# Order of the token operands in the output projection of an encoder step: sums ahead of squares, squares on ScalarE

## The chip, the cores and the metric

The kernel runs on one core of a Trainium2 chip. A core has a matrix engine (PE, with its weight loads shown apart as PEld), a vector engine (DVE), an activation engine (ACT), a general engine (POOL) and an engine that issues transfers (SP). Each works through its own list of instructions in order; semaphores hold an instruction until what it needs is there. Matmuls write to banks of PSUM, everything else lives in SBUF. The metric is the device time of one execution in microseconds, as the median of several runs.

## The reference

One layer of an encoder for 512 prompt frames behind 16 meta tokens, and 64 frames of a running stream. What matters here is the second half of the layer:

```python
mix = jnp.concatenate([o_d.reshape(B, L, D_DIFF), o_m.reshape(B, L, D_MLA)], axis=-1)
x = x + mix @ lp['w_out']
h = rmsnorm(x, lp['norm_ffn_g'])
x = x + (jax.nn.silu(h @ lp['ffn_w_gate']) * (h @ lp['ffn_w_up'])) @ lp['ffn_w_down']
```

`D_MODEL` is 2048, `D_FF` 5632, all in float32. After the meta tokens are dropped, 576 tokens (64 + 512) go through this part.

## The kernel before

Tokens lie along the free dimension, channels on the 128 partitions. A float32 product is made of three products of a faster format (fp32r): every operand is split into a high part (a cast on ACT) and a low part (source minus high part, a subtraction on DVE). `split` and `operand` issue such a pair of instructions.

The program has three phases. Streams of projections and attention come first; the output projection's first half (`mix_out`) runs among them. The third phase begins with the output projection's second half: 16 iterations `i`, one for each block of 128 channels of x, each of 2 half-iterations with 4 weight chunks. A half-iteration loads a 128x512 block of `w_out` (`wr`), splits it (`wh` on ACT, `wl` on DVE; two buffers each, fetched two half-iterations ahead), and runs 24 matmuls (`mm3`, line 205): for each chunk `wh` times `mh`, `wh` times `ml`, `wl` times `mh`, over two halves of 288 tokens. Here `mh` and `ml` are the split attention outputs. At the end of an iteration DVE adds the two sums to `x`, ACT makes `xg`, x scaled by the gain of the next norm, POOL squares x and accumulates the squares in `sq2` (lines 1198 to 1201), and SP stores x.

The feed-forward part that follows uses a Winograd scheme: a product of 2x2 blocks takes 7 products instead of 8. For it, each pair of channel blocks (iterations 2m and 2m+1, eight pairs m) needs seven operands of 128x288: four are quarters of the two `xg` or sums of them, and all seven are split. `token_operands` (line 1048) writes them down once the odd iteration's `xg` is there: operands 1, 2 and 3 are the quarters b11, b21 and b22; 5 is b12 - b11, 6 is b22 - 5, 4 is b21 - 6, 7 is b22 - b12. POOL makes the sums (lines 1060 to 1072, tiles `bs`), in place, so that a sum waits until the one before it has been split. The operands stay in SBUF as tiles `b{p}_{m}` of the pool `bc`.

Behind the loop, `winograd` (matmuls at lines 1155 and 1159) makes the first gate product over pairs 0 to 3 and then over pairs 4 to 7, in the order of products 1, 2, 4, 5, 6, 3, 7; the weights' sums come from POOL (line 1124) and DVE, and `wh`, `wl` again from ACT and DVE. The memory of its weight tiles is that of `mh` and `ml`, which the loop releases.

The order on PE is the order in which the program is written. ACT, DVE and POOL in this stage are not pinned: the framework's scheduler places their instructions by its own estimates of when they become ready, so the order in the program is only one of its inputs. Helpers record one line for all their instructions (125 for ACT, DVE and SP), so tiles tell them apart.

Of the kernel before, what the change touches and what calls it, by code (L numbers as in the profile page):

```python
# [11 lines left out]
F32 = mybir.dt.float32  # L12
F32R = mybir.dt.float32r
AF = mybir.ActivationFunctionType
ALU = mybir.AluOpType
# [4 lines left out]
P = 128  # L20
# [7 lines left out]
TQ = NS + SEQ  # L28
QH = TQ // 2
# [102 lines left out]
def encoder_step(  # L132
# [8 lines left out]
    V, S, Q, G = Engine(tc, nc.vector), Engine(tc, nc.scalar), Engine(tc, nc.sync), nc.gpsimd  # L141
# [10 lines left out]
    def load(dst, src):  # L152
        Q.dma_start(dst, src)

    def store(dst, src):
        Q.dma_start(dst, src)
# [8 lines left out]
    def f32(ap):  # L165
        return ap.bitcast(F32)
# [20 lines left out]
    def weights(src, kcs, cols, dup=False, pool=None):  # L187
        pool = pool or wp
        wr = pool.tile([P, kcs, cols], F32, name="wr", tag="wr", bufs=WR_BUFS)
        if dup:  # L190
            half = cols // 2
            for i in range(2):
                load(wr[:, :, i * half:(i + 1) * half], src)
        else:
            load(wr, src)
        wh = pool.tile([P, kcs, cols], F32R, name="wh", tag="wh", bufs=WH_BUFS)
        wl = pool.tile([P, kcs, cols], F32R, name="wl", tag="wl", bufs=WH_BUFS)
        split(wh, wl, wr)
        return wh, wl

    def mm3(outs, wh, wl, xh, xl, start, stop):
        n = len(outs)
        for p, (w, x) in enumerate(((wh, xh), (wh, xl), (wl, xh))):
            for i in range(n):
                PE.matmul(outs[i], w, x[i], start=start and p == 0, stop=stop and p == 2)  # L205

    def halves(ap):
        n = ap.shape[1] // 2
        return [ap[:, 0:n], ap[:, n:2 * n]]
# [131 lines left out]
    with ExitStack() as ph:  # L341
# [33 lines left out]
        with tc.tile_pool(name="xn", bufs=1) as xn, tc.tile_pool(name="xc", bufs=1, side="right") as xc:  # L375
# [127 lines left out]
            for j, (o, n) in enumerate(tok):  # L503
                b = o // TH
# [507 lines left out]
    def pool(name, side="left"):  # L1012
        cm = tc.tile_pool(name=name, bufs=1, side=side)
        return cm.__enter__(), lambda: cm.__exit__(None, None, None)

    bc, close_bc = pool("bc", "right")
    rw, close_rw = pool("rw", "right")
    sq2 = rw.tile([P, TQ], F32, name="sq2", tag="rows", bufs=2)
    rb2 = rw.tile([P, TQ], F32, name="rb2", tag="rows", bufs=2)
    operands = {}  # L1020
    ORDER = (1, 2, 4, 5, 6, 3, 7)
# [6 lines left out]
    def pin(ins):  # L1028
        if pinned[0]:
            tc.keep_in_program_order(ins)  # L1030
# [3 lines left out]
    def operand_tile(m, p):  # L1034
        b = bc.tile([P, 2, QH], F32R, name=f"b{p}_{m}")
        operands[m, p] = (b[:, 0, :], b[:, 1, :])
        return b

    def operand(m, p, src):
        operand_tile(m, p)  # L1040
        hi, lo = operands[m, p]
        pin(S.activation(hi, src, AF.Copy))
        pin(V.tensor_tensor(lo, src, f32(hi), op=ALU.subtract))

    def quarters(b1, b2):
        return b1[:, 0:QH], b1[:, QH:TQ], b2[:, 0:QH], b2[:, QH:TQ]

    def token_operands(pool, m, b1, b2):

        b11, b12, b21, b22 = quarters(b1, b2)  # L1050

        def sum_tile():
            return pool.tile([P, QH], F32, name="bs", tag="bs", bufs=2)

        operand(m, 1, b11)
        yield
        operand(m, 2, b21)
        yield
        t = sum_tile()
        pin(G.tensor_tensor(t, b12, b11, op=ALU.subtract))  # L1060
        operand(m, 5, t)
        yield
        pin(G.tensor_tensor(t, b22, t, op=ALU.subtract))
        operand(m, 6, t)
        yield
        pin(G.tensor_tensor(t, b21, t, op=ALU.subtract))
        operand(m, 4, t)
        yield
        operand(m, 3, b22)
        yield  # L1070
        t = sum_tile()
        pin(G.tensor_tensor(t, b22, b12, op=ALU.subtract))
        operand(m, 7, t)
        yield

    def load_raw(pool, src, r0, nk, c0, bufs, tag="raw"):
        r = pool.tile([P, nk, 256], F32, name="raw", tag=tag, bufs=bufs)
        load(r, src[r0:r0 + nk * P, c0:c0 + 256].rearrange("(k p) c -> p k c", p=P))
        return r
# [3 lines left out]
    def pmt():  # L1083
        return pm.tile([P, 512], F32, name="m", tag="m")
# [80 lines left out]
    ma, close_ma = pool("ma", "right")  # L1165
    mx, close_mx = pool("mx")
    mixh, mixl = [], []
    for h in range(H):
        m = ma.tile([P, TQ], F32, name="x", tag="x", bufs=3)
# [3 lines left out]
        split(mixh[h], mixl[h], m)  # L1173
    ws = {}

    def fetch(n):
        if n < 2 * KC:
            i, r0 = n // 2, 1024 + n % 2 * 512
            ws[n] = weights(w_out[r0:r0 + 512, i * P:(i + 1) * P].rearrange("(k p) c -> p k c", p=P), 4, P, pool=ma)

    for n in range(2):
        fetch(n)
    for i in range(KC):
        x = ma.tile([P, TQ], F32, name="x", tag="x", bufs=3)
        load(x, x1spill[i])
        ps = [pmt()[:, 0:QH] for _ in range(2)]
        for hf in range(2):
            wh, wl = ws.pop(2 * i + hf)
            for k in range(4):
                mm3(ps, wh[:, k, :], wl[:, k, :],  # L1190
                    halves(mixh[4 * hf + k]), halves(mixl[4 * hf + k]), hf + k == 0, hf + k == 4)
            fetch(2 * i + hf + 2)
        for xi, pi in zip(halves(x), ps):
            V.tensor_tensor(xi, xi, pi, op=ALU.add)
        xg = ma.tile([P, TQ], F32, name="xg", tag="xg", bufs=2)
        S.activation(xg, x, AF.Copy, scale=gF[:, i:i + 1])
        if i == 0:
            G.tensor_tensor(sq2, x, x, op=ALU.mult)
        else:
            G.tensor_tensor(rb2, x, x, op=ALU.mult)  # L1200
            G.tensor_tensor(sq2, sq2, rb2, op=ALU.add)
        store(x2spill[i], x)
        if i % 2:
            for _ in token_operands(ma, i // 2, xe, xg):
                pass
        xe = xg
        if i == 2:
            raw0 = load_raw(rw, w_gate, 0, 8, 0, 1)

    close_mx()  # L1210
    fr, close_fr = pool("fr")
# [161 lines left out]
    for u in range(FC // 2):  # L1373
        out = {}
        for which, wsrc in (("g", w_gate), ("u", w_up)):
            first = turn == 0
            raws = []
            for hf in range(2):
                if turn:
                    rp, bufs = (rw, 1) if turn % 3 == 0 else (fr, 2)  # L1380
# [57 lines left out]
        if u < FC // 2 - blocks[-1]:  # L1438
            b11, b12, b21, b22 = quarters(w[:, 0, :], w[:, 1, :])
            t = g.rearrange("p f (h c) -> p (f h) c", h=2)  # L1440
# [117 lines left out]
    for bi, n in enumerate(blocks):  # L1558
# [32 lines left out]
        else:  # L1591
# [6 lines left out]
            sums, free = itertools.cycle(free[0:3]), free[3:]  # L1598
# [93 lines left out]
```

## Time and profile before

| | |
|---|---|
| median of 3 runs | 2481.91 us (2481.80 to 2481.93) |
| the profiled execution | 2478.58 us, span 2476.8 us |
| PE busy over the span | 2409.9 us (97%) |
| POOL busy over the span | 733.8 us (30%) |
| the projection's second half | about 842.7 to 959.3 us of the span |
| first gate product | from 960.1 us |

In the rows of a timeline the columns are start and length in microseconds, engine, line, operation, output and inputs by the program's names, shapes and count; brackets hold the idle time just before on that engine and what ended it. In the waits the columns are who waited for whom, the total in microseconds, how often, and the longest. In rows of groups they are busy time and mean nanoseconds of one, and idle time before. `PE m L205` are the projection's matmuls, `wl<-wr,wh` a weight's low part, `b<-xg` and `b<-bs` an operand's parts.

### The profile page before, as it was taken

What the parts mean: (1) busy time and instruction counts of PE and PEld (TensorE: products, weight loads), DVE (VectorE), ACT (ScalarE), POOL (GpSimd) and SP (SyncE); (2) the same over time, 40 slices, a digit from 0 to 9 for tenths busy, and PEclk for the clock granted to TensorE, in tenths of its full rate; (3) what the DMA queues carried; (4) which work ended last, traced back from release to release, by engine and by line L of the source; (5) the groups of instructions that cost most, each with busy time, mean ns of one, the idle gap of its engine ahead of it and who ended that gap; (6) DMA issues with size and microseconds to landing.
All of it is one profiled execution on the core that took longest, in us unless ns stands there. A gap on an engine that the chain in (4) does not pass through costs nothing.

```text
span 2476.8 us, 44895 instructions
## 1 busy us (share of the span) xinstructions
PE 2409.9 (97%) x17697; PEld 2364.3 (95%) x17697; DVE 1781.8 (72%) x2831; ACT 1159.4 (47%) x2212; POOL 733.8 (30%) x590
## 2 busy tenths in 40 slices
PE   8999999999999999999999999999999999999998
PEld 6999999988999888999999999999999999999998
DVE  5555555556556567778878888788787988888874
ACT  5444444334444444445555455555554433333345
POOL 0000000000000165554555545545444322222223
PEclk9999999999999999999999999999999999999999
DMA  7533222334232454324444344334443965645332
GB/s 218 146 93 85 82 81 79 89 92 149 85 100 80 148 157 134 120 96 144 155 136 142 129 146 160 128 133 147 141 158 127 310 218 191 228 154 176 105 111 86
DMA packets 336485, 338.05 MB, mean 136 GB/s; under 512 B 25827, under 2 KB 279658, under 8 KB 336274
## 3 DMA queue, kind: packets, MB, share of 16 engines
q1 hardware_dynamic: 335714, 333.12, 42.1%
q8 instruction: 139, 2.28, 0.4%
q0 software_dynamic: 560, 2.06, 0.2%
q14 instruction: 72, 0.59, 0.1%
HBM read 265.21 MB, written 72.61 MB: 136 GB/s over the span
## 4 chain that ended last, share of the span: by engine, by line
PE 58%; DVE 1%; POOL 1%; DMA 1%; ACT 0%; issue 0%; DVEq 0%; POOLq 0%; SPq 0%
PE m L1155 38%; PE m L1159 19%; PE m L205 1%; DMA raw<-in_ffn_w_down 1%; DVE b L125 0%; PE m L1522 0%; DVE wl L125 0%; ACT b L125 0%; POOL b L1509 0%; POOL ws L1124 0%; POOL c L1327 0%; PE m L1536 0%; POOL b L1504 0%; ACT y L125 0%; DVE y L125 0%
## 5 line engine op out<-in xcount | busy, mean ns | idle before, releaser
L1155 PE MATMUL m<-b,wh 128*128 128x288 f32 x7168 | 1048.6, 295 | 4.9 <-ACT wh L125 2.6
L1155 PEld LDWEIGHTS m<-b,wh 128*128 128x128 f32 x7168 | 984.4, 189 | 7.3 <-ACT wh L125 4.9
L1159 PE MATMUL m<-b,wl 128*128 128x288 f32 x3584 | 579.3, 297 | 2.2 <-DVE wl L125 2.2
L1124 POOL TENSOR_TENSOR ws<-raw 128x512 f32<-128x512 f32 (+1 forms) x258 | 367.4, 1432 | 546.0 <-DVE wl L125 289.0
L1159 PEld LDWEIGHTS m<-b,wl 128*128 128x128 f32 x3584 | 513.6, 188 | 3.2 <-DVE wl L125 3.2
L125 ACT ACTIVATE wh<-ws 128x512 fp32r<-128x512 f32 (+1 forms) x340 | 283.5, 846 | 394.8 <-PE m L1155 250.4
L125 DVE TENSOR_TENSOR wl<-ws,wh 128x512 fp32r<-128x512 f32 (+1 forms) x340 | 388.8, 1154 | 93.8 <-ACT wh L125 93.5
L125 DVE TENSOR_TENSOR wl<-raw,wh 128x512 fp32r<-128x512 f32 x387 | 359.0, 953 | 7.5 <-ACT wh L125 6.6
L125 ACT ACTIVATE wh<-raw 128x512 fp32r<-128x512 f32 x387 | 227.4, 620 | 286.9 <-PE m L1155 264.6
L108 PE MATMUL ps<-xh,wh 128*128 128x296 f32 x960 | 221.8, 313 | 3.5 <-ACT wh L125 3.5
L108 PE MATMUL ps<-xh,wl 128*128 128x296 f32 x960 | 211.4, 302 | 0.9 <-DVE wl L125 0.7
L108 PE MATMUL ps<-xl,wh 128*128 128x296 f32 x960 | 211.3, 302 | 0.0
L125 DVE TENSOR_TENSOR y<-y,m 128x288 f32<-128x288 f32 x312 | 140.2, 451 | 89.1 <-PE m L1159 69.5
L108 PEld LDWEIGHTS ps<-xh,wh 128*128 128x128 f32 x960 | 157.8, 192 | 7.9 <-ACT wh L125 4.2
L108 PEld LDWEIGHTS ps<-xh,wl 128*128 128x128 f32 x960 | 157.7, 191 | 1.8 <-DVE wl L125 1.8
L108 PEld LDWEIGHTS ps<-xl,wh 128*128 128x128 f32 x960 | 158.2, 191 | 0.0
L125 DVE TENSOR_TENSOR ws<-ws,raw 128x512 f32<-128x512 f32 (+1 forms) x129 | 112.1, 872 | 63.7 <-POOL ws L1124 61.4
L125 DVE TENSOR_TENSOR wl<-wr,wh 128x1024 fp32r<-128x1024 f32 (+1 forms) x110 | 119.2, 1084 | 34.9 <-ACT wh L125 33.3
L125 ACT ACTIVATE wh<-wr 128x1024 fp32r<-128x1024 f32 (+1 forms) x110 | 101.7, 929 | 55.8 <-PE ps L108 47.5
L1327 POOL TENSOR_TENSOR c<-c,rb 128x576 f32<-128x576 f32 x44 | 70.9, 1612 | 168.6 <-ACT c L125 168.6
L598 POOL MEMSET bias<- 64x64 f32 x8 | 1.2, 144 | 382.8 <-DMA bias<-tsk 274.1
L1435 POOL TENSOR_TENSOR c<-c 128x576 f32<-128x576 f32 x42 | 73.8, 1757 | 85.1 <-DVE c L125 81.3
(342 smaller groups left out, 3161.7 us busy)
## 6 DMA issues: line engine op xcount, KB each, us to landing
raw<-in_ffn_w_gate SPq DMA_DIRECT2D x44, 1024.0 KB, 6.7
raw<-in_ffn_w_up SPq DMA_DIRECT2D x44, 1024.0 KB, 6.9
raw<-in_ffn_w_down SPq DMA_DIRECT2D x39, 1024.0 KB, 6.0
partspill<-parts SPq DMA_DIRECT2D x126, 288.0 KB, 2.1
b<-partspill SPq DMA_DIRECT2D x126, 288.0 KB, 6.0
wr<-in_w_in SPq DMA_DIRECT2D x60, 512.0 KB, 4.0
wr<-in_w_out SPq DMA_DIRECT2D x16, 512.0 KB, 4.1
wr<-in_w_out SPq DMA_DIRECT2D x32, 256.0 KB, 3.8
```

The source lines that it names most:

```text
L108: self.tc.keep_in_program_order(self.pe.matmul(out, lhsT, rhs, start=start, stop=stop))
L125: ins = issue(*args, **kwargs)
L205: PE.matmul(outs[i], w, x[i], start=start and p == 0, stop=stop and p == 2)
L598: G.memset(bias[0:64, 464:528], -BIG)
L1124: engine.tensor_tensor(w[:, k:k + m, :], pick(xs), pick(ys), op=op)
L1155: PE.matmul(banks[p], wh[:, k, :], x, start=first and new and k == 0 and x is hi, stop=False, skip_group_check=not new)
L1159: PE.matmul(banks[p], wl[:, k, :], hi, start=False, stop=last and k == n - 1, skip_group_check=not new)
L1327: G.tensor_tensor(g[:, f, :], g[:, f, :], rb2, op=ALU.mult)
L1435: G.tensor_tensor(w[:, f, :], w[:, f, :], g[:, f, :], op=ALU.mult)
```

## The change

`token_operands` first issues all four sums, into four tiles of their own, and then hands out the seven splits one at a time. Pair m's sums are issued in the odd iteration, ahead of that iteration's squares; its splits are taken two at a time in the half-iterations of the next two iterations, behind the fetch of the next weights. The square of x moves from POOL to ACT (`AF.Square`); the accumulation of the squares stays on POOL. Room for the sums and for `xg` of even pairs comes from the tiles that pair 7's operands will fill later (`last_rooms`); only pair 7's own sums are in tiles of the pool `ma`.

```diff
-    def token_operands(pool, m, b1, b2):
+    def token_operands(m, b1, b2, t5, t6, t4, t7):
 
         b11, b12, b21, b22 = quarters(b1, b2)
...
+        G.tensor_tensor(t5, b12, b11, op=ALU.subtract)
+        G.tensor_tensor(t6, b22, t5, op=ALU.subtract)
+        G.tensor_tensor(t4, b21, t6, op=ALU.subtract)
+        G.tensor_tensor(t7, b22, b12, op=ALU.subtract)
         yield
+        for p, src in ((1, b11), (2, b21), (3, b22), (5, t5), (6, t6), (4, t4), (7, t7)):
+            operand(m, p, src)
+            yield
...
+    def last_room(p):
+        return bc.tile([P, 2, QH], F32, name=f"b{p}_7")
+
+    last_rooms = {p: last_room(p) for p in ORDER[:6]}
+    making = iter(())
...
             fetch(2 * i + hf + 2)
+            for _ in range(2):
+                next(making, None)
         for xi, pi in zip(halves(x), ps):
             V.tensor_tensor(xi, xi, pi, op=ALU.add)
-        xg = ma.tile([P, TQ], F32, name="xg", tag="xg", bufs=2)
+        m = i // 2
+        if m % 2:
+            xg = ma.tile([P, TQ], F32, name="xg", tag="xg", bufs=2)
+        else:
+            xg = last_rooms[1 + i % 2].rearrange("p a b -> p (a b)")
         S.activation(xg, x, AF.Copy, scale=gF[:, i:i + 1])
-        if i == 0:
-            G.tensor_tensor(sq2, x, x, op=ALU.mult)
-        else:
-            G.tensor_tensor(rb2, x, x, op=ALU.mult)
+        if i % 2:
+            if m < 7:
+                sums = [last_rooms[p][:, m % 2, :] for p in (5, 6, 4, 3)]
+            else:
+                sums = [ma.tile([P, QH], F32, name="bs", tag="bs", bufs=4) for _ in range(4)]
+            making = token_operands(m, xe, xg, *sums)
+            next(making)
+        S.activation(sq2 if i == 0 else rb2, x, AF.Square)
+        if i:
             G.tensor_tensor(sq2, sq2, rb2, op=ALU.add)
         store(x2spill[i], x)
-        if i % 2:
-            for _ in token_operands(ma, i // 2, xe, xg):
-                pass
         xe = xg
...
+    for _ in making:
+        pass
```

What the scheduler makes of it shows in the lists of instructions. First ACT, for pair 1 (iterations 2 and 3), from the odd iteration's `xg` on; `b_1_...` are the pair's operands, here 2, 3, 6, 7 and then 4, and the two `wh` are the high parts of the weights for the third and fourth half-iteration of the next pair. Before:

```order
L125 ACTIVATE xg<-x,gT 128x576
L125 ACTIVATE b_1_9799<-xg 128x288
L125 ACTIVATE b_1_9815<-xg 128x288
L125 ACTIVATE b_1_9808<-bs 128x288
L125 ACTIVATE b_1_9820<-bs 128x288
L125 ACTIVATE wh<-wr 128x512
L125 ACTIVATE b_1_9812<-bs 128x288
L125 ACTIVATE wh<-wr 128x512
```

Operands 6 and 7 stand ahead of the third half-iteration's weights. In the change, the same place, where `b_7_9476`, `b_7_9474` and `b_7_9477` are the rooms of the sums for operands 6, 4 and 7, and `rb_9414` is the square:

```order
L125 ACTIVATE xg<-x,gT 128x576
L125 ACTIVATE rb_9414<-x 128x576
L125 ACTIVATE b_1_9839<-xg 128x288
L125 ACTIVATE b_1_9872<-xg 128x288
L125 ACTIVATE b_1_9918<-b_7_9476 128x288
L125 ACTIVATE wh<-wr 128x512
L125 ACTIVATE b_1_9921<-b_7_9474 128x288
L125 ACTIVATE b_1_9954<-b_7_9477 128x288
L125 ACTIVATE wh<-wr 128x512
```

The square has come in ahead of operand 2, and one operand (7) has moved from ahead of the third half-iteration's weights to behind them. DVE has the same sequence of operands and weights, without the square. Next POOL, for the same pair, with `bs` the sums for operands 5, 6, 7 and 4. Before:

```order
L1060 TENSOR_TENSOR bs<-xg 128x288
L1200 TENSOR_TENSOR rb_9414<-x 128x576
L1201 TENSOR_TENSOR sq_9413<-sq_9413,rb_9414 128x576
L1063 TENSOR_TENSOR bs<-xg,bs 128x288
L1072 TENSOR_TENSOR bs<-xg 128x288
L1066 TENSOR_TENSOR bs<-xg,bs 128x288
```

The multiplication and the accumulation of the odd iteration stand ahead of the sums for 6, 7 and 4. In the change, for pair 2, whose `xg` lie in the rooms `b_7_9472` and `b_7_9473`:

```order
L1051 TENSOR_TENSOR b_7_9475<-b_7_9472 128x288
L1202 TENSOR_TENSOR sq_9413<-sq_9413,rb_9414 128x576
L1052 TENSOR_TENSOR b_7_9476<-b_7_9473,b_7_9475 128x288
L1054 TENSOR_TENSOR b_7_9477<-b_7_9473,b_7_9472 128x288
L1053 TENSOR_TENSOR b_7_9474<-b_7_9473,b_7_9476 128x288
L1202 TENSOR_TENSOR sq_9413<-sq_9413,rb_9414 128x576
```

The multiplication has left, and the accumulation stands behind the sums instead of ahead of them. Last, ACT at the end of the loop, where `wh<-raw` and `wh<-ws` are gate weights (the row with x2 holds products 1 and 2, the next `wh<-raw` product 4) and `b_7_...` here are operands of pair 7. Before:

```order
L125 ACTIVATE wh<-raw 128x512 x2
L125 ACTIVATE xg<-x,gT 128x576
L125 ACTIVATE wh<-raw 128x512
L125 ACTIVATE b_7_10801<-xg 128x288
L125 ACTIVATE b_7_10810<-bs 128x288
L125 ACTIVATE b_7_10817<-xg 128x288
L125 ACTIVATE b_7_10822<-bs 128x288
L125 ACTIVATE wh<-ws 128x512 x2
L125 ACTIVATE b_7_10814<-bs 128x288
```

Product 4's weights stand ahead of the operands. In the change:

```order
L125 ACTIVATE wh<-raw 128x512 x2
L125 ACTIVATE xg<-x,gT 128x576
L125 ACTIVATE rb_9414<-x 128x576
L125 ACTIVATE b_7_10793<-xg 128x288
L125 ACTIVATE b_7_10796<-xg 128x288
L125 ACTIVATE b_7_10802<-bs 128x288
L125 ACTIVATE b_7_10805<-bs 128x288
L125 ACTIVATE b_7_10808<-bs 128x288
L125 ACTIVATE wh<-raw 128x512
L125 ACTIVATE wh<-ws 128x512 x3
```

Product 4's weights have moved from ahead of the odd iteration's operands to behind all five of them. PE and SP have the same sequence of instructions as before.

More of the change, by code (lines that the diff above doesn't have):

```diff
@@ L1046, in quarters @@
         return b1[:, 0:QH], b1[:, QH:TQ], b2[:, 0:QH], b2[:, QH:TQ]
-    def token_operands(pool, m, b1, b2):
+    def token_operands(m, b1, b2, t5, t6, t4, t7):
         b11, b12, b21, b22 = quarters(b1, b2)
-        def sum_tile():
-            return pool.tile([P, QH], F32, name="bs", tag="bs", bufs=2)
-        operand(m, 1, b11)
+        G.tensor_tensor(t5, b12, b11, op=ALU.subtract)
+        G.tensor_tensor(t6, b22, t5, op=ALU.subtract)
+        G.tensor_tensor(t4, b21, t6, op=ALU.subtract)
+        G.tensor_tensor(t7, b22, b12, op=ALU.subtract)
         yield
[L1057 to L1074, printed above, removed]
+        for p, src in ((1, b11), (2, b21), (3, b22), (5, t5), (6, t6), (4, t4), (7, t7)):
+            operand(m, p, src)
+            yield
     def load_raw(pool, src, r0, nk, c0, bufs, tag="raw"):
```

## The prediction

> **What bounds the kernel now.** I read the page's first part, the waits of the stage, a table of windows, and then one pair of iterations engine by engine.
>
> ```profile
> PE 2409.9 (97%) x17697; PEld 2364.3 (95%) x17697; DVE 1781.8 (72%) x2831; ACT 1159.4 (47%) x2212; POOL 733.8 (30%) x590
> ...
> PE m L205 <- ACT wh L125: 3.4, 6, 0.6
> PE m L205 <- DVE wl L125: 2.7, 8, 0.5
> ...
> ACT b L125 <- POOL bs L1060: 21.0, 8, 3.5
> ACT b L125 <- POOL bs L1063: 19.5, 8, 3.0
> ...
> 864.60:879.19 14.59, 13.57 (x97) 12.71 (x96) 9.16 (x15) 6.64 (x13) 9.68 (x9) 1.00 0.55 170
> ...
> 937.51:952.11 14.60, 13.71 (x96) 12.89 (x97) 9.20 (x16) 6.75 (x13) 9.37 (x9) 1.00 0.44 134
> ```
>
> PE is the bound over the whole span, so only time in which PE stands still can be won. In this stage it stands still for weights: `wh` from ACT, `wl` from DVE. ACT in turn waits 40 us for token sums from POOL. The two window rows (columns: window, length, busy time of PE, PEld, DVE, ACT, POOL with counts, clock, DMA) are the first and the last of six pairs of iterations; 96 matmuls take 14.58 us. What they would take without a stall, and where the stalls are, is in PE's order of time:
>
> ```profile
> 890.91 0.43 PE L205 MATMUL m<-ml,wh 128*128 128x288 f32 x2
> ...
> 892.78 0.42 PE L205 MATMUL m<-mh,wl 128*128 128x288 f32 x2
> 893.76 0.54 PE L205 MATMUL m<-mh,wh 128*128 128x288 f32 x2 [0.56 <-ACT wh L125]
> 894.13 0.43 PE L205 MATMUL m<-ml,wh 128*128 128x288 f32 x2
> 894.87 0.53 PE L205 MATMUL m<-mh,wl 128*128 128x288 f32 x2 [0.31 <-DVE wl L125]
> 895.24 0.43 PE L205 MATMUL m<-mh,wh 128*128 128x288 f32 x2
> ```
>
> From 890.91 to 892.78 seven groups of two take 0.267 each, so 48 groups are 12.77 us, and a pair loses 14.58 - 12.77 = **1.81 us**. I call the four blocks of 24 matmuls in a pair 1 and 2 (even i) and 3 and 4 (odd i). Block 3 wants to start at 892.78 + 0.27 = 893.05 and starts at 893.76 (0.71); its `wl` costs 0.47 more (0.74 instead of 0.27 between starts); each restart takes 0.37 instead of 0.27. The rest, some 0.4, lies at block 1 (rows further down). What holds `wh` of block 3 stands on ACT, POOL and DVE:
>
> ```profile
> 887.80 0.78 ACT L125 ACTIVATE xg<-x,gT 128x576 f32<-128x576 f32 x1 [0.97 <-DVE x L125]
> 888.61 0.78 ACT L125 ACTIVATE b<-xg 128x288 fp32r<-128x288 f32 x2
> 891.98 0.44 ACT L125 ACTIVATE b<-bs 128x288 fp32r<-128x288 f32 x1 [2.59 <-POOL bs L1063]
> 892.75 0.45 ACT L125 ACTIVATE b<-bs 128x288 fp32r<-128x288 f32 x1 [0.32 <-POOL bs L1072]
> 893.10 0.61 ACT L125 ACTIVATE wh<-wr 128x512 fp32r<-128x512 f32 x1
> ...
> 887.90 1.47 POOL L1200 TENSOR_TENSOR rb<-x 128x576 f32<-128x576 f32 x1 [2.59 <-issue]
> 889.45 1.52 POOL L1201 TENSOR_TENSOR sq<-sq,rb 128x576 f32<-128x576 f32 x1
> 890.93 1.02 POOL L1063 TENSOR_TENSOR bs<-xg,bs 128x288 f32<-128x288 f32 x1
> 891.91 0.80 POOL L1072 TENSOR_TENSOR bs<-xg 128x288 f32<-128x288 f32 x1
> ...
> 889.09 2.19 DVE L125 TENSOR_TENSOR b<-xg,b 128x288 fp32r<-128x288 f32 x2 [0.72 <-ACT b L125]
> 892.46 0.57 DVE L125 TENSOR_TENSOR b<-bs,b 128x288 fp32r<-128x288 f32 x1 [1.18 <-ACT b L125]
> 893.22 0.99 DVE L125 TENSOR_TENSOR b<-bs,b 128x288 fp32r<-128x288 f32 x1 [0.20 <-ACT b L125]
> 894.13 0.68 DVE L125 TENSOR_TENSOR wl<-wr,wh 128x512 fp32r<-128x512 f32 x1
> ```
>
> POOL squares first (887.90 to 890.97) and sums afterwards; ACT's casts of operands 6 and 7 wait for the sums, and `wh` stands behind both. The DVE rows show a second thing: a subtraction of 128x288 that takes about 0.45 alone takes longer while POOL works, and ends 0.3 after POOL's instruction (pairs: 893.03 after 892.71, 894.21 after 893.90; the second of the two at 889.09 ends at 891.28, after 890.97). POOL pays less: its sum at 890.93 took 1.02 instead of 0.80.
>
> **The change part by part.** Taken off POOL: 16 multiplications x*x. Added on ACT: 16 squares of 128x576. The trace has that operation elsewhere:
>
> ```profile
> L125 ACT ACTIVATE sq<-o 128x576 f32<-128x576 f32 x8 | 5.4, 677 | 0.1
> ```
>
> 16 x 0.68 = 10.9 us of ACT. ACT is busy 6.6 of 14.6 in the window rows, so this hides unless it stands ahead of a `wh` that is late; it stands ahead of `wh` of block 3, counted below. Without that cover it would cost 0.68 a pair.
>
> The four sums now have tiles of their own and come ahead of the squares' accumulation. They are followed from xg of the odd iteration. Undisturbed, blocks 1 and 2 no longer lose their 0.4: `wh` of block 1 stood behind operand 5, whose sum came after POOL's two square instructions; that sum now starts right behind xg.
>
> ```profile
> 885.99 0.43 PE L205 MATMUL m<-mh,wl 128*128 128x288 f32 x2
> 886.37 0.53 PE L205 MATMUL m<-mh,wh 128*128 128x288 f32 x2
> ...
> 886.35 0.69 DVE L125 TENSOR_TENSOR wl<-wr,wh 128x512 fp32r<-128x512 f32 x1
> 886.96 0.81 DVE L125 TENSOR_TENSOR x<-x,m 128x288 f32<-128x288 f32 x2
> ```
>
> So block 3 wants to start at 893.05 - 0.4 = 892.65, and x is read when block 4's last matmuls end (885.99 + 0.43), at about 886.5 instead of 886.96: DVE no longer has block 1's `wl` in front. In the same clock:
> - xg 887.3 to 888.1 on ACT; POOL's sum for operand 6 888.2 to 889.0, for 7 to 889.8 (0.8 each).
> - ACT: square to 888.7, casts for 2, 3 and 6 to 889.8, and `wh` of block 3 done by 890.5. Wanted at 892.65: the 0.71 is gone. Its weights must have landed; the load is issued behind `wl` of block 1, and lands 3.8 later by the row below, at about 890.6. Then `wh` is done by 891.2, still in time.
>
> ```profile
> L125 SPq DMA_DIRECT2D wr<-in_w_out x29: 383/384/1941, 844.8 to 946.7; - x29
> ...
> DMA to landing us min/median/max: 2.9/3.8/4.8
> ```
>
> - DVE has operands 2, 3 and 6 ahead of `wl` of block 3, and POOL's sums (0.8) and the accumulation (1.52) get in between, one against one: 2 behind the sum for 7 (889.8, done 890.1), 3 behind the sum for 4 (1.0 with the delay, 890.8, done 891.1), 6 behind the accumulation (892.4, done 892.7). Then `wl` takes to 893.35, and PE sees it at 893.41. It wants it 0.53 - 0.13 after block 3 begins, at 893.05. **What is late next is `wl` of block 3**: 0.36 and 0.10 for the restart, 0.45 a pair. Bounds: 0, if one POOL instruction fewer gets in (it is 1.5 us earlier then); 1.4, if one sum more gets in.
>
> Operands 4 and 7 follow behind `wl` of block 3 and end well before block 4 needs its `wl`.
>
> [...]
>
> Sum over the loop. The six pairs lose 6 x 1.81 = 10.9 today. Two stalls lie outside their windows, one of 0.6 in the first pair and one of 0.6 in the last (idle 0.34 and 0.31 by the rows below, which is 0.5 between starts as at 894.87, and 0.1 for the restart). DVE's `wl` is ready earlier at both in the new order, and I take both, 1.2 (bounds 0.6 and 1.2).
>
> ```profile
> 861.76 0.54 PE L205 MATMUL m<-mh,wl 128*128 128x288 f32 x2 [0.34 <-DVE wl L125]
> ...
> 953.22 0.53 PE L205 MATMUL m<-mh,wl 128*128 128x288 f32 x2 [0.31 <-DVE wl L125]
> ...
> 953.24 1.45 POOL L1124 TENSOR_TENSOR ws<-raw 128x512 f32<-128x512 f32 x1 [1.00 <-DVE wl L125]
> ```
>
> Against that stand block 3's new waits: the first pair has `wl` ahead of operand 6 on DVE and none, six pairs have 0.45, 2.7 together. In the last pair POOL's weight sum of 1.45 gets in before operand 7, so `wl` of the last block is some 0.2 late (bounds 0 and 0.6).
>
> **The seam** behind the loop, where gate weights follow, moves too: ACT's split for product 4 stood ahead of five operands of pair 7 and now stands behind them all.
>
> ```profile
> 964.81 0.80 PE L1159 MATMUL m<-b,wl 128*128 128x288 f32 x4
> 967.43 1.32 PE L1155 MATMUL m<-b,wh 128*128 128x288 f32 x8 [1.82 <-ACT wh L125]
> ...
> 972.57 0.80 PE L1159 MATMUL m<-b,wl 128*128 128x288 f32 x4 [0.30 <-DVE wl L125]
> ```
>
> Today product 5 is 2.1 late and product 3 another 0.6. In the new order product 4 waits for `wh` (about 1.9, behind xg, square and five casts) and again for `wl` (about 1.1, behind five DVE subtractions that meet three sums and an accumulation); then products 5, 6 and 3 find theirs ready. That is 3.0 against 2.7 and a small restart: I take 0, bounds a gain of 1.0 and a loss of 1.5. Behind the seam every engine has the same sequence as before.
>
> Total: 10.9 + 1.2 - 2.7 - 0.2 = **9.2 us**. The profiled execution took 2478.58 (span 2476.8), so it would become 2469.4. The median of the runs, 2481.91, stands 3.3 above; it becomes **2472.7**.
>
> **The rivals.**
> [...]
> 2. *All stalls go.* The accumulation comes after operand 6 on DVE: 10.9 + 1.2 - 0.2 = 11.9, so 2470.0. Against: POOL has its turn as soon as operand 3 is through, 1 us before operand 6.
> 3. *The wait only changes its name.* The scheduler puts the splits back near their sums (the order on ACT is nearly the old one), DVE meets the accumulation and one sum more, and `wl` loses 1.4: 10.9 + 1.2 - 8.4 - 0.2 = 3.5, so 2478.4, not to be told from no change. For it: `wl` already loses 0.47 today. Against: the 3.0 us of squares ahead of the sums are gone from POOL.
> 4. *Slower, by the seam.* The split for product 4 stands behind every operand of pair 7. Three `wl` of 0.6 each took 4.08 there, because POOL was squaring:
>
> ```profile
> 960.67 4.08 DVE L125 TENSOR_TENSOR wl<-raw,wh 128x512 fp32r<-128x512 f32 x3
> ```
>
> If each of DVE's five subtractions meets 1.5 of POOL, product 4 is 7.5 late for them alone and not some 3; with the weight sum of 1.45 and one more such meeting before product 5 the seam loses 4.5 + 1.5 + 0.5 = 6.5 more than today. It decides only where the loop wins less than that, so with rival 3's 3.5: 3.0 slower, 2484.9. Against: POOL has just one instruction of 1.5 left in the new order there, and the loop has to fail too.
>
> **How the numbers follow.** Forecast 0.53 (own range 2471 to 2474.5), strict lock 0.20, all gone 0.10, name only 0.12, slower 0.05. A measurement here tells 0.2% (5 us) from no change. Faster: 0.53 + 0.20 + 0.10 = 0.83; same 0.12; slower 0.05. The range 2469.4 to 2478.4 holds the first three cases and the near half of the fourth.
>
> **What would show it.** Right: windows of a pair near 13.2 us; no PE wait for `wh` in the loop, one for `wl` a pair of about 0.35; ACT's waits for POOL's sums near zero; POOL 24 us shorter; at the seam PE waits for product 4 instead of 5. Wrong: pairs above 14 us, PE waiting for `wh`, or a PE wait over 4 us at the seam.

## The result

The changed kernel takes 2470.45 us (median of 5 runs, 2467.77 to 2472.42) against 2481.93 for the kernel before (2481.8 to 2483.55). The ratio is 0.9952, with a 95% interval of 0.9937 to 0.9966: 11.5 us less, where 9.2 were forecast. It is faster by more than 0.2%, and the time lies in the range, 2.3 below the forecast. In a later set of the same kernel one of six executions took 3333.27 us at a granted clock of 0.65; it is left out of the medians and ratios below.

### The profile page after: what moved, and what is told of

The parts are those of the page before. It is cut to its first block, busy times and chain, and to the rows that moved or that the text cites. A ratio compares the mean times of both kernels' runs of the same rounds, so it can differ in the third digit from the quotient of the medians.

```text
span 2470.7 us, 44876 instructions
## 1 busy us (share of the span) xinstructions
PE 2410.5 (98%) x17697; PEld 2370.1 (96%) x17697; DVE 1790.9 (72%) x2831; ACT 1167.5 (47%) x2228; POOL 707.6 (29%) x574
## 4 chain that ended last, share of the span: by engine, by line
PE 70%; DVE 2%; ACT 1%; DMA 1%; issue 1%; POOL 0%; DVEq 0%; ACTq 0%; POOLq 0%; SPq 0%
PE m L1139 38%; PE m L1143 19%; PE ps L108 5%; PE m L205 4%; PE sp L108 1%; PE po L108 1%; DVE b L125 1%; PE tp L112 1%; PE pv L108 1%; DMA raw<-in_ffn_w_down 0%; DVE wl L125 0%; PE m L1522 0%; ACT b L125 0%; DMA wr<-in_w_out 0%; ACT wh L125 0%
```

## The profile after

The first part of the page, and below it what PE and ACT wait for in the stage (who waits for whom, total us, how often, longest):

```profile
PE 2410.5 (98%) x17697; PEld 2370.1 (96%) x17697; DVE 1790.9 (72%) x2831; ACT 1167.5 (47%) x2228; POOL 707.6 (29%) x574
```

```profile
PE m L205 <- DVE wl L125: 1.0, 3, 0.6
...
ACT wh L125 <- DMA wr<-in_w_out: 10.0, 7, 2.9
...
ACT b L125 <- POOL b L1053: 3.6, 6, 0.6
```

POOL has lost 26.2 us. ACT's waits for the sums, 21.0 and 19.5 before, are 3.6. PE has no wait for `wh` in the loop any more; 1.0 us for `wl` is left, all of it in the first pairs. What is new is ACT's 10.0 us of waiting for `wr`, the weights' transfer (2.6 before).

The six pairs, here cut at block 3's first matmul with `wl` (the table of before was cut at the first with `wh`; cut at `wl`, its six pairs take 87.55 instead of 87.51):

```profile
870.38:883.61 13.23, 12.98 (x97) 12.70 (x97) 10.76 (x17) 7.79 (x15) 6.34 (x6) 1.00 0.57 170
883.61:897.22 13.61, 13.05 (x96) 12.82 (x96) 10.48 (x16) 7.46 (x15) 6.36 (x6) 1.00 0.54 165
897.22:910.15 12.93, 12.93 (x96) 12.81 (x97) 10.41 (x16) 7.57 (x15) 6.37 (x6) 1.00 0.59 174
910.15:923.09 12.94, 12.94 (x98) 12.82 (x97) 10.41 (x16) 7.58 (x15) 6.38 (x6) 1.00 0.58 172
923.09:936.03 12.94, 12.94 (x97) 12.83 (x96) 10.39 (x16) 7.80 (x15) 6.37 (x6) 1.00 0.58 174
936.03:949.01 12.98, 12.98 (x97) 12.81 (x97) 10.51 (x16) 7.46 (x15) 6.37 (x6) 1.00 0.50 150
sum 78.63, PE 77.82 PEld 76.80 DVE 62.95 ACT 45.65 POOL 38.19; mean PE 12.97 PEld 12.80 DVE 10.49 ACT 7.61 POOL 6.36
```

They take 78.63 instead of 87.51. A steady pair takes 12.94, 0.14 above the 12.80 that a pair takes where nothing waits ("No odd accumulation" below); the first two are longer. One steady pair on PE, DVE, POOL and ACT:

```profile
903.17 0.43 PE L205 MATMUL m<-mh,wh 128*128 128x288 f32 x2
...
909.84 0.43 PE L205 MATMUL m<-ml,wh 128*128 128x288 f32 x2
910.15 0.53 PE L205 MATMUL m<-mh,wl 128*128 128x288 f32 x2
910.52 0.42 PE L205 MATMUL m<-mh,wh 128*128 128x288 f32 x2
...
903.24 0.82 DVE L125 TENSOR_TENSOR x<-x,m 128x288 f32<-128x288 f32 x2 [0.23 <-PE m L205]
905.81 2.07 DVE L125 TENSOR_TENSOR b<-xg,b 128x288 fp32r<-128x288 f32 x2 [1.15 <-ACT b L125]
907.80 1.69 DVE L125 TENSOR_TENSOR b<-b,b 128x288 fp32r<-128x288 f32 x1
909.42 0.68 DVE L125 TENSOR_TENSOR wl<-wr,wh 128x512 fp32r<-128x512 f32 x1
...
906.54 1.03 POOL L1053 TENSOR_TENSOR b<-xg,b 128x288 f32<-128x288 f32 x1
907.52 1.65 POOL L1202 TENSOR_TENSOR sq<-sq,rb 128x576 f32<-128x576 f32 x1
...
906.35 0.61 ACT L125 ACTIVATE wh<-wr 128x512 fp32r<-128x512 f32 x1
```

ACT has `wh` of block 3 at 906.96, 2.6 before block 3. On DVE the two operands at 905.81 meet POOL's sums. Operand 6 at 907.80, which takes about 0.45 alone, meets the accumulation (907.52 to 909.17) and ends at 909.49, 0.32 after it. `wl` ends at 910.10, and PE, due at 910.11, starts at 910.15.

**Where the profiled time went.** The profiled execution took 2472.42 (span 2470.7), 6.1 less in span than that of before:

| stretch | before | after | difference |
|---|---|---|---|
| start to the first matmul of this stage | 842.73 | 848.32 | +5.6 |
| this stage, to its last matmul | 116.18 | 106.37 | -9.8 |
| from there to product 1 over pairs 4 to 7 | 15.88 | 16.36 | +0.5 |
| from there to the end of the span | 1502.0 | 1499.65 | -2.35 |

The first stretch has the same instructions in both kernels; its 5.6 belong to the execution, and the last section comes back to them. That is why this profile shows 6.1 while the medians differ by 11.5.

## The experiments

Theory: POOL's order set the pair. With the squares off POOL and the sums ahead, `wh` is early, and what is left is DVE's chain of operands 2, 3 and 6 ahead of `wl`, stretched by the POOL instructions it meets. Rivals: only one part of the change matters; the handing out of splits doesn't matter; what is left in a pair is ordinary. Each kernel ran beside the kernel before on the same chip (medians of before 2480.5 to 2481.9). "Loop end to end" is from the stage's last matmul to the end of the span. As shown further down, the edit "gate load later" moves no instruction: that row is the change once more, and "both of these" is "last splits later" once more.

| kernel | steady pair | PE waits in it for | loop end to end | median us | ratio to before, 95% |
|---|---|---|---|---|---|
| before | 14.58 | `wh` 0.56, `wl` 0.31 | 1517.9 | 2481.93 | |
| the change | 12.94 | 0.04 | 1516.0 | 2470.45 | 0.9952 (0.9937 to 0.9966) |
| squares on ACT alone | 13.23 | `wl` 0.19 | 1515.7 | 2473.70 | 0.9969 (0.9958 to 0.9981) |
| sums first, squares on POOL | 14.37 | `wh` 0.55 | 1519.1 | 2480.47 | 0.9997 (0.9988 to 1.0007) |
| splits at once | 13.68 | `wl` 0.62 | 1516.0 | 2476.48 | 0.9984 (0.9974 to 0.9994) |
| accumulation twice | 14.15 | `wl` 1.1 | 1519.2 | 2481.85 | 1.0003 (0.9994 to 1.0012) |
| no odd accumulation | 12.80 | none | 1516.2 | 2469.43 | 0.9952 (0.9940 to 0.9965) |
| last splits later | 12.93 | 0.04 | 1516.4 | 2469.12 | 0.9957 (0.9945 to 0.9970) |
| gate load later | 12.93 | 0.04 | 1516.3 | 2469.14 | 0.9949 (0.9937 to 0.9962) |
| both of these | 12.93 | 0.04 | 1517.7 | 2468.60 | 0.9946 (0.9932 to 0.9959) |
| the change again | 12.94 | 0.04 | 1516.8 | 2470.94 | 0.9962 (0.9949 to 0.9975) |
| odd accumulation on DVE, gate load later | 12.80 | none | 1516.7 | 2468.30 | 0.9949 (0.9938 to 0.9961) |
| all three moves | 12.80 | none | 1517.1 | 2468.33 | 0.9950 (0.9938 to 0.9962) |

### Squares on ACT alone

```diff
 (the kernel before)
-            G.tensor_tensor(sq2, x, x, op=ALU.mult)
+            S.activation(sq2, x, AF.Square)
...
-            G.tensor_tensor(rb2, x, x, op=ALU.mult)
+            S.activation(rb2, x, AF.Square)
```

> The kernel before with only the squares moved to ACT; the sums stay in place on POOL and the splits where they were. Theory (POOL's 3 us of squaring ahead of the sums held the weights): POOL's sum for operand 6 starts right behind xg, wh of block 3 is in time, wl of block 3 is 0.3 to 0.4 late, a pair takes 13.2 to 13.4 us instead of 14.58, and the time is 7 to 8 below before (2474 to 2475). Rival (it is the order of sums and splits that counts): pairs stay above 14 us and the time within 3 of 2481.9.

A pair falls to 13.23 and the time to 2473.7: this part alone brings 1.35 of the 1.64 that a steady pair gains. The timeline of one pair:

```profile
903.31 1.68 DVE L125 TENSOR_TENSOR b<-bs,b 128x288 fp32r<-128x288 f32 x1
904.92 0.45 DVE L125 TENSOR_TENSOR b<-xg,b 128x288 fp32r<-128x288 f32 x1
905.29 1.06 DVE L125 TENSOR_TENSOR b<-bs,b 128x288 fp32r<-128x288 f32 x1
906.27 0.68 DVE L125 TENSOR_TENSOR wl<-wr,wh 128x512 fp32r<-128x512 f32 x1
...
903.03 1.65 POOL L1201 TENSOR_TENSOR sq<-sq,rb 128x576 f32<-128x576 f32 x1
905.07 0.96 POOL L1066 TENSOR_TENSOR bs<-xg,bs 128x288 f32<-128x288 f32 x1 [0.40 <-DVE b L125]
```

Four operands instead of three stand ahead of `wl`. One meets the accumulation; the last meets POOL's sum for operand 4, which came late because, in place, it had to wait until operand 6 was split.

### Sums first, squares on POOL

```diff
 (the changed kernel)
-        S.activation(sq2 if i == 0 else rb2, x, AF.Square)
+        G.tensor_tensor(sq2 if i == 0 else rb2, x, x, op=ALU.mult)
```

> The changed kernel with the squares back on POOL, behind the sums. Theory (DVE's subtractions alternate with POOL's instructions one against one): operands 6 and 7 now meet the multiplication and the accumulation of 1.5 us each, so wl of block 3 is about 1.9 late, a pair takes 14.5 to 14.9 us and the time is within 2 of before. Rival (sums ahead of squares is what won): a pair takes about 13 us and the time stays near 2471.

14.37 and 2480.47: not to be told from before. The timeline of ACT and POOL says why:

```profile
908.16 0.45 ACT L125 ACTIVATE b<-b 128x288 fp32r<-128x288 f32 x1 [2.59 <-POOL b L1052]
908.92 0.45 ACT L125 ACTIVATE b<-b 128x288 fp32r<-128x288 f32 x1 [0.32 <-POOL b L1054]
909.27 0.61 ACT L125 ACTIVATE wh<-wr 128x512 fp32r<-128x512 f32 x1
...
904.08 1.47 POOL L1200 TENSOR_TENSOR rb<-x 128x576 f32<-128x576 f32 x1 [2.59 <-issue]
905.63 1.52 POOL L1202 TENSOR_TENSOR sq<-sq,rb 128x576 f32<-128x576 f32 x1
907.11 1.02 POOL L1052 TENSOR_TENSOR b<-xg,b 128x288 f32<-128x288 f32 x1
```

The sums are written ahead of the square, and stand behind it all the same: the square needs x, the sums need `xg`, which ACT makes from x 0.8 later, and the scheduler seems to give POOL what is ready first. So the expected cause, a `wl` that is 1.9 late behind operands meeting the squares, did not come, and a pair is a little below the 14.5 expected; PE waits for `wh` as before. To write the sums first brings 0.2 a pair unless the square has left the engine.

### Splits handed out at once

```diff
 (the changed kernel)
-            next(making)
+            for _ in making:
+                pass
```

> The changed kernel with all seven splits issued at once behind the sums, none handed out in later half-iterations. On ACT and DVE operands 4 and 7 then stand ahead of block 3's weights instead of behind. Theory: wl of block 3 loses 0.7 to 0.9 a pair, a pair takes 13.6 to 13.8 us, and the time is 5 above the changed kernel (2475 to 2476). Rival (the scheduler undoes the handing out, it has no effect): the same as the changed kernel, 12.93 a pair.

13.68 and 2476.48. The two rows of DVE in a pair:

```profile
909.27 2.42 DVE L125 TENSOR_TENSOR b<-b,b 128x288 fp32r<-128x288 f32 x3
911.62 0.68 DVE L125 TENSOR_TENSOR wl<-wr,wh 128x512 fp32r<-128x512 f32 x1
```

Operands 6, 4 and 7 now all stand ahead of `wl` of block 3 (2.42 instead of 1.69 for one), and PE waits 0.62 a pair for it. So the order behind the next weights is worth 0.74 of a steady pair. The time is 0.5 above the range expected; the first of the six pairs was longer too, 15.0, and the one before it 16.2.

### Accumulation twice

```diff
 (the changed kernel)
             G.tensor_tensor(sq2, sq2, rb2, op=ALU.add)
+            if i % 2:
+                G.tensor_tensor(sq2, sq2, rb2, op=ALU.add)
```

> The changed kernel with POOL's accumulation of the odd iterations done twice (the sum of squares is then too large, so that y is scaled otherwise). Theory (a DVE subtraction waits for POOL's whole instruction): wl of block 3 meets the second accumulation, ends 1.4 to 1.6 later, and a pair takes 14.3 to 14.6 us instead of 12.93: about 9 above the changed kernel, 2479 to 2481. Rival (POOL off the path costs nothing, PE waits for something else): 12.93 a pair and 2470.5.

1.5 us more on POOL in a place where POOL is idle afterwards cost 1.2 of the pair (14.15, just below the range expected), and with 3.2 more behind the loop, where the last pair's accumulation is doubled too, the whole gain. In the timeline `wl` itself now meets the second accumulation, and PE waits:

```profile
909.02 1.51 POOL L1204 TENSOR_TENSOR sq<-sq,rb 128x576 f32<-128x576 f32 x1
...
909.18 1.90 DVE L125 TENSOR_TENSOR wl<-wr,wh 128x512 fp32r<-128x512 f32 x1
...
911.14 0.53 PE L205 MATMUL m<-mh,wl 128*128 128x288 f32 x2 [1.12 <-DVE wl L125]
```

`wl` takes 0.68 elsewhere; here it ends at 911.08, 0.55 after POOL's 910.53.

### No odd accumulation

```diff
 (the changed kernel)
-        if i:
+        if i and i % 2 == 0:
             G.tensor_tensor(sq2, sq2, rb2, op=ALU.add)
```

> The changed kernel, but the squares of the odd channel blocks are not added to the sum of squares, so POOL loses the accumulation that stands behind the four sums (the norm's sum then holds the even blocks only). Theory: what is left of the stall in a steady pair (12.93 to 12.98 against 12.77 without any) is that accumulation meeting DVE's subtraction for operand 6 ahead of wl of block 3. So steady pairs take 12.77 to 12.82, without any PE wait for wl; six pairs gain about 1 us, and the time is 2469 to 2470. Rival: the 0.16 is something else (ordinary restarts of PE), and pairs stay at 12.93 or more. In the first pairs, where weights arrive late, both expect no change.

12.80 in every pair, no wait; the windows (two of the pairs):

```profile
908.74:921.54 12.80, 12.80 (x98) 12.80 (x97) 9.24 (x15) 7.68 (x16) 4.75 (x5) 1.00 0.59 175
921.54:934.34 12.80, 12.80 (x98) 12.80 (x97) 9.24 (x15) 7.68 (x16) 4.75 (x5) 1.00 0.58 176
```

So the rest of the stall is the accumulation meeting operand 6. The time, 2469.43, can't be told from the change's; the windows can. One thing was not expected: the first pairs are 12.8 too.

### Last splits later, gate load later, and both

```diff
 (the changed kernel; last splits later)
-    for _ in making:
-        pass
...
     winograd(fw, ma, [raw0], range(4), None, banks0, stag=("wr", WR_BUFS))
+    for _ in making:
+        pass
```

```diff
 (the changed kernel; gate load later)
-        if i == 2:
+        if i == 8:
             raw0 = load_raw(rw, w_gate, 0, 8, 0, 1)
```

> The changed kernel, but what is left of the last pair's splits is written down behind the first gate product over pairs 0 to 3, so that product 4's weights stand ahead of them on ACT. Theory: at the seam PE waited for product 4's weights only because of the order on ACT and DVE (1.84 for wh, 0.22 for wl, and a clock of 0.79 for 8 us behind it, about 1.7). All of that goes: from the loop's last matmul to product 1 over pairs 4 to 7 it takes 12.5 to 14 instead of 16.4, and the time is 2466 to 2469. Rival: the operands of pair 7 are then late for products over pairs 4 to 7, or the sums from POOL and weights' sums take the place, and a wait of about 2 comes back within 15 us: 2470 to 2472.

> The changed kernel, but the load of the first gate weights (1 MB) is written down in iteration 8 instead of 2. Theory: the two longer pairs (13.3 and 13.75 at 883 and 897) come from that load: it delays the projection's own weights, so that wh and wl are late. Those pairs become 12.9, and the delay shows up two to three pairs later or not at all, if the queue then has fewer other transfers: a gain of up to 1.1, 2469.3 to 2470.5. Rival: weights are late there for another reason (x and its stores), and the same two pairs stay at 13.3 to 13.8.

> The changed kernel with both: the last pair's splits behind the first gate product, and the gate load in iteration 8. If both theories hold the gains add up: the seam 12.5 to 14, no pair above 13.2, and 2465 to 2468. If neither holds it is the changed kernel's 2470.5.

Three misses, each by little in time. With the last splits later PE no longer waits for `wh` of product 4, and from the loop's last matmul to product 1 over pairs 4 to 7 it takes 13.9 instead of 16.4 (15.3 where the change had no dip of the clock there, as told further down). But 36 us on PE stands still again, longer than in the change (1.28 there), and the clock falls behind it; the timeline, and the window (the clock is the third number from the end):

```profile
1000.50 1.34 PE L1143 MATMUL m<-b,wl 128*128 128x288 f32 x8 [1.98 <-DVE wl L125]
```

```profile
1000.00:1008.00 8.00, 7.50 (x45) 7.50 (x46) 7.97 (x11) 2.63 (x5) 5.42 (x4) 0.79 0.10 37
```

From the loop's end to the end of the span it is 1516.4, as in the change (1516.0 and 1516.8): the seam's gain was given back.

The edit for the gate load does not move the load. Its transfer on SP, in the kernel with the edit and then in the change:

```profile
850.99 0.43 SPq L125 DMA_DIRECT2D raw<-in_ffn_w_gate  x1
853.79 0.32 SPq L125 DMA_DIRECT2D x2spill<-x  x1
```

```profile
856.23 0.43 SPq L125 DMA_DIRECT2D raw<-in_ffn_w_gate  x1
859.36 0.32 SPq L125 DMA_DIRECT2D x2spill<-x  x1
```

In both it is issued ahead of the first iteration's store of x, 8.7 and 7.9 us after the stage's first matmul (842.26 and 848.32). The two programs have the same instructions in the same order on every engine: the scheduler, not the line in the text, places the load. So whether the gate load makes the first pairs longer was not tested. What the runs do show is how far these pairs move by themselves. The last pair ahead of the six windows and the first two of the six took 12.86, 13.23 and 13.61 in the change, 12.52, 12.85 and 13.39 when it ran again, and 13.98, 12.98 and 13.04 here, with the same instructions. The pair of 13.98 ends with this row:

```profile
865.94 0.53 PE L205 MATMUL m<-mh,wl 128*128 128x288 f32 x2 [1.32 <-DVE wl L125]
```

"Both of these" is then last splits later a second time: 13.9 at the seam and 1.98 at the later wait again, and 2468.60 after 2469.12. Three sets of the change have medians of 2470.45, 2470.94 and 2469.14, so no gain from the later splits shows.

### The change again, odd accumulation on DVE, and all three moves

```diff
 (the changed kernel, with the gate load written down in iteration 8)
-            G.tensor_tensor(sq2, sq2, rb2, op=ALU.add)
+            (V if i % 2 else G).tensor_tensor(sq2, sq2, rb2, op=ALU.add)
```

> The changed kernel itself, to set the versions beside it on the same chip: 2468 to 2473, steady pairs 12.9 to 13.0, and 1.75 to 1.85 of PE waiting for product 4's weights at the seam. What it tells apart is how far the first pairs and the clock dips (0.79 for 8 us) move by themselves: a first pair that is now shorter or longer than 13.2 to 13.8, or a seam without a dip, shows that they are no part of the order of instructions.

> The changed kernel with the odd iterations' accumulation of the squares on DVE (0.76 there) instead of POOL, where it stands ahead of operand 2, and with the gate load in iteration 8. Theory: DVE's subtraction for operand 6 then meets no POOL instruction, wl of block 3 is ready about 0.8 earlier although DVE has 0.76 more ahead of it, and every steady pair takes 12.77 to 12.85, as it does where the accumulation is left out (12.80). The loop takes 104 to 106 and the time is 2467 to 2469.5. Rival: the accumulation on DVE meets the sums for operands 7 and 4 itself, DVE stands 0.3 to 1.0 longer, and wl is as late or later: pairs 12.95 to 13.3, 2470 to 2472.

> The kernel with the odd accumulation on DVE and the late gate load, and the last pair's splits behind the first gate product too. Earlier run: that edit shortened the seam (from the loop's last matmul to product 1 over pairs 4 to 7 took 13.9 instead of 15.3 to 16.4), but a wait for wl 36 us later grew from 1.28 to 1.98, with the clock at 0.79 for 8 us behind it. Theory: that wait is set by a chain through POOL and DVE that does not start earlier, so it is 1.9 to 2.1 here too and the seam's gain is given back: the time is that of the same kernel without this edit, within 1. Rival: the gain adds up, 1.5 to 3 below it.

The change again has steady pairs of 12.94 and waits 1.83 for product 4's `wh`, as expected.

Since the gate load stays where it was, the kernel with the odd accumulation on DVE has that move alone, and "all three moves" are two. With the odd accumulation on DVE the pairs are 12.80 without a wait; a window and the timeline of that pair:

```profile
912.74:925.53 12.79, 12.79 (x98) 12.79 (x97) 10.00 (x16) 7.67 (x16) 5.27 (x5) 1.00 0.55 163
```

```profile
915.04 0.96 DVE L125 TENSOR_TENSOR sq<-sq,rb 128x576 f32<-128x576 f32 x1 [0.81 <-ACT rb L125]
915.92 2.41 DVE L125 TENSOR_TENSOR b<-b,b 128x288 fp32r<-128x288 f32 x3
918.25 0.68 DVE L125 TENSOR_TENSOR wl<-wr,wh 128x512 fp32r<-128x512 f32 x1
```

DVE does one thing more ahead of `wl` and is done with it sooner: accumulation and three operands take 3.3 (915.04 to 918.33), where the three operands alone took 3.7 beside POOL's accumulation (905.81 to 909.49 above). Its median, 2468.30, is the lowest of all, but only the windows tell it from the changed kernel: that took 2470.94 beside it, the intervals of the two ratios (0.9938 to 0.9961, 0.9949 to 0.9975) overlap, and another set of the change had the same ratio, 0.9949. All three moves together take the same, 2468.33, with the later wait of 1.99 that was expected.

## Why the prediction was right, and where it was off

- **PE the bound, 1.81 lost in a pair, by `wh` behind the sums.** Right. `wh` waits are gone, and putting the square back on POOL brings them back (0.55) with 14.37. The size is 0.03 high: seven groups in 1.87 us make 12.82 for 48, not 12.77, and pairs in which nothing waits take 12.80.
- **"What is late next is `wl` of block 3", 0.45 a pair.** The place and the cause are right: one accumulation more gives 1.1 of waiting, none gives 0. The size was 0.14 (12.94 - 12.80): 0.04 of idle and 0.10 for the restart (910.15 to 910.52 instead of 0.27), where 0.36 and 0.10 were forecast. Two readings made up the difference. I let DVE read x 0.24 after block 1's start in an undisturbed pair (886.5 against 885.99 + 0.27); the rows show 0.07 (903.24 after 903.17). And I let PE want `wl` 0.40 after block 3 begins; it wants it 0.54 after (909.57 to 910.11, two groups of two). Together 0.31 of the 0.32.
- **Six pairs lose 2.7.** They lost 78.63 - 6 x 12.80 = 1.8. Six times 0.14 is 0.8 of that. The other 1.0 lies in the first two pairs, where `wr` came late, which was no term of the sum: on ACT a `wh` waits 2.92 for `wr` up to 890.64, xg stands behind it, and with xg the sums, the operands and `wl` start later (PE waits 0.56 at 897.22). The rerun has one such pair (13.39). So the sum came near partly by luck: the wait was put too high, and a delay that nobody had counted filled part of the gap.
- **Two stalls of 0.6 outside the windows, 1.2.** Both are gone in this profile; in the rerun 0.41 of idle stands at the second place again (block 3 of the last pair). The 0.2 for the last block's `wl` did not come in either.
- **The seam, 0.** The change of places came as told: product 4 waits for `wh` and `wl`, and products 5, 6 and 3 find theirs. The rows, and the later wait behind them:

```profile
961.14 1.67 PE L1139 MATMUL m<-b,wh 128*128 128x288 f32 x8 [1.84 <-ACT wh L125]
963.02 1.33 PE L1143 MATMUL m<-b,wl 128*128 128x288 f32 x4 [0.22 <-DVE wl L125]
...
1005.86 1.33 PE L1143 MATMUL m<-b,wl 128*128 128x288 f32 x8 [1.28 <-DVE wl L125]
```

  1.84 was forecast as 1.9. The 0.22 was forecast as 1.1, but it is short because PE itself was slow there (product 4's eight matmuls with `wh` take 1.67 instead of 1.32); in the other two executions of the same instructions it is 0.56 and 0.55. The stretch to product 1 over pairs 4 to 7 took 16.36, 16.84 and 15.32 in the three, and 15.88 before. Behind the waits of 1.84 and 1.83 in the first two the clock fell to 0.79 for 8 us, behind the 1.85 in the third it stayed up. So the new order alone gains 0.6 at the seam, inside the bounds, and a dip, which no term held, costs 1.0 to 1.5 there.
- **"Behind the seam every engine has the same sequence as before."** True of the order, not of the time. Before, the wait at this later place was 1.87 and the clock fell behind it; the windows of before and of the change there:

```profile
1008.00:1016.00 8.00, 6.13 (x35) 5.90 (x34) 7.66 (x11) 1.95 (x4) 4.07 (x4) 0.79 0.10 37
```

```profile
960.00:968.00 8.00, 6.64 (x38) 6.30 (x39) 7.25 (x10) 3.79 (x7) 2.96 (x3) 0.79 0.59 195
1000.00:1008.00 8.00, 6.72 (x51) 6.48 (x50) 5.38 (x7) 2.31 (x4) 4.30 (x4) 1.00 0.25 81
```

  In these two profiles the change moved one dip from there to the seam, and made the later wait 0.6 shorter; 2.35 came from that stretch. The wait is 1.29 and 1.28 in the other two executions, again without a dip, and from the loop's end to the end of the span the three take 1516.0, 1516.8 and 1516.3 against 1517.9 before: 1.1 to 1.9 us were won where the sum had 0, with one profile of before to compare.
- **The rivals.** The chances give 0.20 to a "strict lock"; no run shows one. What the rows show in its place is that POOL's own instructions under DVE took 1.03 and 1.65 instead of 0.81 and 1.43, 0.2 longer each, while DVE's operand 6 took 1.69 instead of 0.45 and ended 0.32 after POOL's accumulation. With all stalls gone nothing of the wait would be left; 0.14 is near to that. That the wait only changes its name comes nearest with the splits handed out at once (0.88 a pair instead of 1.4), not here. No PE wait at the seam came near 7.5.

The step that was mis-sized is thus the new wait (0.14 instead of 0.45 a pair). 9.8 us went from the stage (116.18 to 106.37) where 9.2 were forecast: 8.9 instead of 8.2 in the six windows, and 0.9 instead of 1.0 outside them. That the medians differ by 11.5 and not by 9.8 fits what was won behind the loop, and is within the interval of the ratio (8.4 to 15.6 us).

## What to carry to other kernels

An engine that is hardly half busy (here, before the change, POOL at 30% of the span and ACT at 47%) can still set the pace through the order of its instructions: ask what stands ahead of the one that somebody waits for, and move that to an engine that doesn't share its wait, rather than rewrite the order and hope that the scheduler keeps it. Look in the trace whether an edit moved what it was meant to move, before its time is read as an answer: the one for the gate load moved nothing. In these rows a DVE operation that met a POOL instruction ended 0.31 to 0.55 after it (operand 6 took 1.69 instead of 0.45, `wl` 1.90 instead of 0.68): cost it by the end of the POOL instruction that it meets, not by its own length. An operation more on DVE can be cheaper than one on POOL beside it (3.3 with the accumulation on DVE against 3.7 with it on POOL). A gain that moves a stall along (here by 36 us) is not a gain: compare from a point behind the next stall.

## What the runs showed of the hardware that was not expected

- **A short wait can cost clock.** Among the waits at and behind the seam, each of 1.9 us or more (1.94, 1.98, 1.98, 1.99, 2.79) had the clock down behind it. Behind 1.98 and 1.99 the granted clock was 0.79 over 8 us (0.98 and 0.81 in two such windows behind the other 1.98), behind 1.94 it was 0.92 and 0.87 in two; each is an estimated 1.7 us, the sum of 8 us times what was missing to 1. Behind 2.79 eight matmuls took 2.29 instead of 1.32. Behind 1.28, 1.52 and 1.58 it stayed up. In between it went both ways: a dip after 1.76, 1.83, 1.84, 1.85 (with a wait of 1.75 close behind it) and 1.87, none after 1.76, 1.82 and 1.85. Three of these (1.83, 1.84 and the 1.85 without a dip) are one place in three executions of the same instructions, so the length of the wait does not decide it alone. At the start of the stage, where several shorter waits stand close together, a dip followed 1.54, and none 1.48. So under two us of waiting, with work on both sides, was enough for a dip in these rows (1.76 to 1.99). What decides between a dip and none was not shown.
- **The same instructions took 842.3 to 848.3 us up to this stage**, over the thirteen profiles, whose instructions up to there have the same order. The dips of the clock lie at other places in each: in the change's profile at 72 to 88, 400 to 416 and 832 to 856 us, which were undisturbed or less so before. By the granted clock in windows of 8 us they cost, up to the last matmul, an estimated 24 us in the change and 14 before. So the span of a single profile can't show a gain below some 6 us here, while windows of a steady pair repeat within 0.06.
- **What stays open.** In the first pairs `wr` sometimes lands late, and the same instructions take up to 14.0 us there instead of 12.8 (up to 14.5 with the last splits later, a kernel that has the same order there). Whether that is the gate load, the phase of the transfers or what precedes the stage was not settled: no kernel here has the load at another place.
